# Two fp32r token parts in place of three bf16 ones for the experts' gather, a reordered router, and the late modulation's columns by 32-wide sums

## The chip, the cores and the metric

The kernel runs on one core of one Trainium2 chip. A core has the matrix engine TensorE (PE in the profile, with its weight loads as PEld), VectorE (DVE), ScalarE (ACT), GpSimd (POOL) and SyncE (SP), which issues almost all transfers. The metric is the time of one execution on the device in microseconds (us). It is compared as a median of runs.

## The reference

One block of a diffusion model over 256 latent tokens of width 1024, with 256 context tokens:

```python
m_lat = ada_mod(c, ada_w, ada_b)            # silu(c) @ w + b: six rows of 1024
h_lat = modulate(rms_norm(x, norm1_g), m_lat[0], m_lat[1])
y_lat = token_mixers(h_lat, h_ctx, ...)     # retention and latent attention, merged, @ w_out
x  = x + m_lat[2] * y_lat                   # gate 1
h2 = modulate(rms_norm(x, norm2_g), m_lat[3], m_lat[4])
x  = x + m_lat[5] * moe(h2, router_w, router_b, w_gu, b_gu, w_down, b_down)
return rms_norm(x, final_norm_g)

def moe(tok, ...):
    logits = tok @ router_w + router_b      # 32 experts
    top_val, top_idx = lax.top_k(logits, 4); gates = softmax(top_val)
    # each expert: gu = xb @ w_gu + b_gu; ((up + 1) * gate * sigmoid(1.702 * gate)) @ w_down + b_down
    # its tokens' outputs are weighted by the gates and added
```

All weights and activations are float32. Each of the 32 experts reads 12.6 MB of weights, some 403 MB in all.

## The kernel before, in words

**The order of work.** The kernel is one long list of `step`s, written out by hand, and the order in the list is the order on every engine. A step may name a weight tile. `run_steps` then loads that tile through SP, up to seven tiles (`WR`) ahead, into a ring of 512 KB tiles. Most products outside the experts are made of three fp32r products (fp32r is a 4-byte format of reduced precision, which the matrix engine takes directly). ACT and DVE split a weight tile into a high and a low fp32r part (`split`, lines 276 and 277, tile `ws`), two tiles ahead of its use. `mm3` (lines 285 to 287) multiplies high by high, high by low, low by high.

**The front (to about 545 us).** First comes the early modulation with the first projections, then four pairs of attention heads. In a pair, `scores` is followed by `attend_rows` (transposes of the probabilities on PE, split by ACT and DVE into `pth`/`ptl` and `kn`) and `attend` (their products with the values). The list goes on with the attention's branch product (`w_branch_mla`), four retention heads, their branch products, and `w_out`. In between lie 32 steps of `more_ada`. Each loads 512 KB of the late modulation's weights and adds them into the tile `ada` by one DVE instruction (line 340). `ada` then holds 128 partial rows that still have to be summed over the partitions.

**The late modulation (`gates`).** PE sums over the partitions by a product with ones. Two rows come out as copies on all partitions (lines 1190 and 1195: `gate1`, `gate2`). The shift and scale rows are wanted as columns, and 16 products of one column each make them (line 1201). `router_weights` folds them into the router's weights (line 1210).

**The router.** `residual(c)` makes half `c` of the new `x` on DVE. `x2_rows(c)` squares it (ACT), transposes it (PE) for the router's product (`router(c)`, line 1289), and starts the split of `x` into three bf16 parts (`split3`): ACT rounds and POOL subtracts, twice. `keep_warm` is idle work for PE. After that DVE alone works through a chain: the norm's inverse root (`rsqrt`), the logits `lgt`, the top four (`sel`, `eq`, the scan `cum`, `selb`), the tokens' positions `posm`, and a 0/1 matrix `oh` that says which token sits in which of an expert's 64 slots.

**The experts.** Weights come through a second ring of ten 2 MB tiles. Three open late in the retention (`open_ring`), one in `close_early`, five when the front's memory is given back, and the last when the pool `tmp` is. Per expert PE runs `gate_up` (line 1479, four tiles), `slot_rows` (line 1448), for every second expert `slot_scale` (line 1411), one `gather` (line 1426: `oh` times the three parts of `x`, for a later pair of experts), the transposes of the activation (line 145), `gu_bias` (line 1340), `down` (line 1510, two tiles), and `combine` (line 1459). The activation itself is a chain DVE, ACT, DVE (lines 1483 to 1487) between `gate_up` and those transposes.

Of the kernel before, what the change touches and what calls it, by code (L numbers as in the profile page):

```python
# [59 lines left out]
def hybrid_block(ctx: ExitStack, tc: tile.TileContext, A, out, dbg=None):  # L60
# [68 lines left out]
    identb = cst.tile([128, 128], BF, name="identb")  # L129
    nc.vector.tensor_scalar(identb, jp, 0.0, None, op0=OP.is_equal)  # L130
# [1024 lines left out]
    def open_late():  # L1155
# [13 lines left out]
        O["x3"] = late.tile([128, 2, D], BF, name="x3")  # L1169
# [11 lines left out]
    def open_out():  # L1181
        ret.close()
        dump("merged", M["acc"])
        O["tmp"] = enter(tmps, "tmp", side="right", reuse_waits="tile")

    def gates():
        mod2 = O["mod2"]
        for i in range(2):
            ps = pt_()
            nc.tensor.matmul(ps, one32[:, 0:1].to_broadcast([128, 128]), ada[:, 0, 512 * i:512 * i + 512],  # L1190
                             start=True, stop=True)
            nc.scalar.activation(O["gate1"][i], ps, AF.Copy)
        ps = pt_()
        for i in range(2):
            nc.tensor.matmul(ps[64 * i:64 * i + 64], one32[:, 0:1].to_broadcast([128, 64]),
                             ada[:, 1, 1024 + 512 * i:1536 + 512 * i], start=True, stop=True)
# [5 lines left out]
        nc.vector.scalar_tensor_tensor(mod2[:, 0], pc[:, 0], 1.0, g2c, op0=OP.add, op1=OP.mult)  # L1202
        nc.vector.tensor_copy(mod2[:, 1], pc[:, 1])
# [43 lines left out]
    def x2_rows(c):  # L1247
        x, tmp = O["x"], O["tmp"]
        cs = slice(512 * c, 512 * c + 512)
        if c == 0:  # L1250
            O["s2"] = O["late"].tile([128, 2, 2], F32, name="s2")
            x12 = accp.tile([128, 2, 2, D], BF, name="acc_m")
            O["xs"] = x12[:, 0], x12[:, 1], O["x3"]
# [4 lines left out]
        for t in range(2):  # L1258
# [3 lines left out]
            dst = tmp.tile([128, 4, 128], F32, name="x2T", bufs=2)  # L1262
            if c:
                nc.vector.tensor_copy(dst, ps)
            else:
                nc.scalar.activation(dst, ps, AF.Copy)
            O["x2T", c, t] = dst
        for t in range(2):
            O["split", c, t] = split3([p[:, t, cs] for p in O["xs"]], x[:, t, cs],
                                      tmp.tile([128, 512], F32, name="rest", bufs=2))  # L1270

    def split3(parts, src, rest):

        nc.scalar.activation(parts[0], src, AF.Copy)
        nc.gpsimd.tensor_tensor(rest, src, parts[0], op=OP.subtract)

        def more():
            nc.scalar.activation(parts[1], rest, AF.Copy)
            nc.gpsimd.tensor_tensor(parts[2], rest, parts[1], op=OP.subtract)
        return more  # L1280

    def split_more(c):
        for t in range(2):
            O["split", c, t]()

    def router(c):
        for t in range(2):
# [15 lines left out]
    step(lambda: router(0))  # L1303
    step(lambda: split_more(0))
# [6 lines left out]
    split_more(1)  # L1311
# [20 lines left out]
    r23 = late.tile([128, 3, 2], BF, name="r23")  # L1332
    split3([r23[:, i] for i in range(3)], r2, late.tile([128, 2], F32, name="r2r"))()
# [41 lines left out]
    keep_warm(CLK[7])  # L1375
    posm = late.tile([128, 2, E], F32, name="posm")
    nc.vector.scalar_tensor_tensor(posm, pp[:, 0:2], 1.0, selb, op0=OP.add, op1=OP.mult)
    nc.vector.tensor_scalar(posm, posm, -1.0, None, op0=OP.add)
    def oh_tile():
        return late.tile([128, 2, EG, CAP], BF, name="oh", bufs=2)  # L1380

    oh0 = oh_tile()
    one_hot(oh0, posm[:, :, 0:EG], EG)

# [20 lines left out]
    def slot_scale(oh, ne):  # L1405
# [3 lines left out]
        for t in range(2):  # L1409
            for i in range(3):  # L1410
                nc.tensor.matmul(ps[:, :w], r23[:, i, t:t + 1].to_broadcast([128, 128]),
                                 oh[:, t, :ne].rearrange("p e s -> p (e s)"), start=(t + i == 0), stop=(t + i == 3))
# [4 lines left out]
    def gather(oh, rb, xg, k4, ne):  # L1417
# [3 lines left out]
        for t in range(2):  # L1421
            rhs = oh[:, t, :ne].rearrange("p e s -> p (e s)")
            for p, part in enumerate(xs):
                for i in range(4):
                    k = 4 * k4 + i
                    nc.tensor.matmul(ps[:, i, :w], pairs(part[:, t], 4)[:, k // 2, k % 2], rhs, start=(t + p + i == 0), stop=(t + p == 3),  # L1426
                                     skip_group_check=True)
# [14 lines left out]
    def slot_rows(oh, i):  # L1442
# [3 lines left out]
        for t in range(2):  # L1446
            for h in range(2):
                nc.tensor.matmul(ps[64 * h:64 * h + 64, 128 * t:128 * t + 128], oh[:, t, i], identb,
# [265 lines left out]
```

## Time and profile before

| What | Value |
|---|---|
| median of 3 runs | 1489.52 us (1488.69 to 1493.41) |
| the profiled execution's own time | 1487.58 us |
| its span, first to last instruction | 1485.8 us |
| PE busy | 1388.0 us (93%) |
| DVE, ACT, POOL busy | 651.5, 344.4, 87.9 us |
| the chain that ended last | PE 51%, DMA 40%, DVE 6% of the span |
| traffic | 492.38 MB, mean 331 GB/s |
| mean granted clock of TensorE | 0.988 of full speed |

All times inside the kernel are counted from the span's start. The own time is 1.8 us longer than the span, which is what lies around it. The shares are means over two very different stages, the front and the experts, so each stage is read by itself. A matmul's busy time in the trace includes a modelled end, so the pace of a stream of matmuls is read from the distance between starts.

### The profile page before, as it was taken

The page shows a single profiled execution, that of the slowest core. Times are in us where ns is not written, and L with a number is a line of the kernel's source. Part 1 is how long each engine was busy: PE and PEld are TensorE (multiplying, and loading weights), DVE is VectorE, ACT ScalarE, POOL GpSimd, SP SyncE. Part 2 cuts the span into 40 slices and gives each one's busy share as a digit, 9 for nine tenths or more (in the row PEclk, how much of TensorE's full clock was granted, in tenths as well). Part 3 has the DMA queues.
Part 4 walks back from the last instruction along what each step waited for, and adds up shares of the span by engine and source line. Part 5 has one row for each costly group of instructions (what it writes and reads, how often), then busy time and mean ns, then how long its engine had stood idle before and what let it go on. Part 6 is the DMA issues. An engine that isn't in the chain of part 4 may idle for free.

```text
span 1485.8 us, 18943 instructions
## 1 busy us (share of the span) xinstructions
PE 1388.0 (93%) x7859; PEld 775.8 (52%) x7859; DVE 651.5 (44%) x1111; ACT 344.4 (23%) x604; POOL 87.9 (6%) x95
## 2 busy tenths in 40 slices
PE   8998999999999989999999999989899889989986
PEld 4677888888888874333333333333333333333323
DVE  4488876757676572323322323222322232223224
ACT  4364543534443331110100101100110011001001
POOL 2201050101101030000000000000000000000000
PEclk9999999999999899999999999999999999999998
DMA  8634473554548778999999999999999999999994
GB/s 286 204 108 141 142 265 101 164 177 130 176 161 322 266 286 337 427 426 427 428 425 428 427 426 427 427 428 426 427 428 426 428 427 427 427 428 427 427 422 172
DMA packets 75077, 492.38 MB, mean 331 GB/s; under 512 B 6579, under 2 KB 16892, under 8 KB 50152
## 3 DMA queue, kind: packets, MB, share of 16 engines
q1 hardware_dynamic: 74008, 489.22, 81.8%
q0 software_dynamic: 576, 1.23, 0.3%
q8 instruction: 63, 1.03, 0.3%
q10 hardware_dynamic: 400, 0.66, 0.1%
q14 instruction: 30, 0.25, 0.0%
HBM read 490.03 MB, written 1.05 MB: 331 GB/s over the span
## 4 chain that ended last, share of the span: by engine, by line
PE 51%; DMA 40%; DVE 6%; issue 1%; ACT 1%; POOL 0%; SPq 0%; DVEq 0%; ACTq 0%
DMA w<-in_exp_w_gu_dram 26%; DMA w<-in_exp_w_down_dram 13%; PE ps L1479 11%; PE ps L286 9%; PE ps L287 9%; PE ps L285 9%; PE ps L1510 5%; PE ps L145 2%; PE ps L1340 1%; PE ps L308 1%; PE ps L1459 1%; PE ps L457 1%; DVE up L1487 1%; DVE up L1485 1%; DVE ws L277 0%
## 5 line engine op out<-in xcount | busy, mean ns | idle before, releaser
L1479 PE MATMUL ps<-w,xg 128*64 128x512 f32 x2048 | 459.8, 596 | 36.2 <-DMA w<-in_exp_w_gu_dram 33.9
L1479 PEld LDWEIGHTS ps<-w,xg 128*64 128x64 f32 x2048 | 140.5, 137 | 333.8 <-issue 253.7
L1510 PE MATMUL ps<-w,ga 128*64 128x512 f32 x992 | 218.1, 592 | 0.0
L277 DVE TENSOR_TENSOR ws<-w,ws 128x1024 fp32r<-128x1024 f32 (+2 forms) x114 | 139.2, 1230 | 66.4 <-ACT ws L276 65.3
L1466 DVE SCALAR_TENSOR_TENSOR x<-ps,gate,x 128x512 f32<-128x512 f32 x124 | 84.5, 744 | 187.2 <-PE ps L1459 187.2
L1510 PEld LDWEIGHTS ps<-w,ga 128*64 128x64 f32 x992 | 71.2, 137 | 141.9 <-issue 141.9
L1519 DVE TENSOR_TENSOR ps<-ps,gate 128x512 f32<-128x512 f32 (+1 forms) x33 | 22.6, 683 | 270.1 <-PE ps L1510 261.2
L276 ACT ACTIVATE ws<-w 128x1024 fp32r<-128x1024 f32 (+2 forms) x114 | 116.9, 1028 | 101.0 <-PE ps L287 79.5
L1484 ACT ACTIVATE ps<-ga 128x512 f32<-128x512 f32 x32 | 19.3, 602 | 471.5 <-DVE ga L1483 471.5
L286 PE MATMUL ps<-ws,hh 128*128 128x512 f32 (+3 forms) x304 | 109.5, 360 | 3.5 <-DVE ws L277 3.5
L285 PE MATMUL ps<-ws,hh 128*128 128x512 f32 (+3 forms) x304 | 110.1, 362 | 2.4 <-DVE ptl L282 2.4
L287 PE MATMUL ps<-ws,hl 128*128 128x512 f32 (+3 forms) x304 | 109.1, 359 | 0.4 <-DVE hl L383 0.4
L1483 DVE TENSOR_SCALAR ga<-ps 128x512 f32<-128x512 f32 x32 | 22.1, 692 | 161.4 <-PE ps L1479 161.4
L281 ACT ACTIVATE up<-ps 128x512 fp32r<-128x512 f32 (+1 forms) x33 | 19.3, 584 | 260.2 <-DVE ps L1519 260.1
L286 PEld LDWEIGHTS ps<-ws,hh 128*128 128x128 f32 x304 | 57.3, 188 | 13.2 <-DVE ws L277 4.9
L1340 PE MATMUL ps<-bgu,ident 128*64 128x512 f32 x256 | 63.2, 615 | 0.0
L285 PEld LDWEIGHTS ps<-ws,hh 128*128 128x128 f32 x304 | 57.1, 188 | 11.4 <-DVE ptl L282 2.7
L287 PEld LDWEIGHTS ps<-ws,hl 128*128 128x128 f32 x304 | 57.1, 188 | 9.1 <-DVE hl L383 0.7
L145 PE MATMUL ps<-ident,up 128*128 128x128 f32 x128 | 24.1, 312 | 24.0 <-DVE up L1487 24.0
L340 DVE SCALAR_TENSOR_TENSOR ada<-w,sc,ada 128x1024 f32<-128x1024 f32 x32 | 40.6, 1278 | 0.0
L1426 PE MATMUL ps<-oh,acc_m 128*128 128x128 bf16 x512 | 40.6, 224 | 0.0
L285 PE MATMUL ps<-ath,hth 128*128 128x256 f32 x128 | 35.7, 279 | 1.2 <-ACT ath L281 1.2
(383 smaller groups left out, 1820.5 us busy)
## 6 DMA issues: line engine op xcount, KB each, us to landing
w<-in_exp_w_gu_dram SPq DMA_DIRECT2D x124, 2048.0 KB, 39.1
w<-in_exp_w_down_dram SPq DMA_DIRECT2D x62, 2048.0 KB, 39.1
w<-in_ada_w_dram SPq DMA_DIRECT2D x48, 512.0 KB, 4.5
w<-in_w_in_dram SPq DMA_DIRECT2D x48, 512.0 KB, 4.5
w<-in_w_in_dram SPq DMA_DIRECT2D x32, 256.0 KB, 4.3
w<-in_w_branch_ret_dram SPq DMA_DIRECT2D x16, 512.0 KB, 5.9
w<-in_exp_w_gu_dram SPq DMA_DIRECT2D x8, 1024.0 KB, 27.1
w<-in_w_branch_mla_dram SPq DMA_DIRECT2D x8, 512.0 KB, 5.2
```

The lines of the kernel that those rows point to most:

```text
L145: nc.tensor.transpose(dst, src, ident[:n, :n])
L276: nc.scalar.activation(hi[:, :n], src, AF.Copy)
L277: nc.vector.tensor_tensor(lo[:, :n], src, hi[:, :n].bitcast(F32), op=OP.subtract)
L285: nc.tensor.matmul(ps, a[0], b[0], start=start, stop=False, skip_group_check=True)
L286: nc.tensor.matmul(ps, a[0], b[1], start=False, stop=False, skip_group_check=True)
L287: nc.tensor.matmul(ps, a[1], b[0], start=False, stop=stop, skip_group_check=True)
L340: nc.vector.scalar_tensor_tensor(a, w, sc[:, k:k + 1], a, op0=OP.mult, op1=OP.add)
L1340: nc.tensor.matmul(ps[64 * h:64 * h + 64], pick_row(c // 512).to_broadcast([128, CAP]), bgu, start=True, stop=False, skip_group_check=True)
L1426: nc.tensor.matmul(ps[:, i, :w], pairs(part[:, t], 4)[:, k // 2, k % 2], rhs, start=(t + p + i == 0), stop=(t + p == 3), skip_group_check= ...
L1466: nc.vector.scalar_tensor_tensor(a, pss[h], g[:, t:t + 1], a, op0=OP.mult, op1=OP.add)
L1479: nc.tensor.matmul(ps[64 * h:64 * h + 64], xg[k // 4][:, k % 4, sl], w[:, c:c + 512], start=False, stop=(k == KD - 1), skip_group_check=True)
L1510: nc.tensor.matmul(py[64 * h:64 * h + 64], hT[f], w[:, 1024 * r + 512 * h:1024 * r + 512 * h + 512], start=(f == 0), stop=(f == KD - 1))
```

## The change

**Gather.** `x` is kept as two fp32r parts, `acc_m` (high, in place of two bf16 parts) and a new tile `xlo` (low, 8 KB per partition in place of 4 KB for `x3`). The subtraction is a DVE instruction; POOL no longer takes part. `oh` and the inverse norm's parts `r2s` are fp32r too. A `gather` has 16 products in place of 24, a `slot_scale` 4 in place of 6. `slot_rows` multiplies by the float32 identity.

**Router.** The squares, the transposes and the router's products of half 0 are interleaved with the transposes of half 1; ACT makes all four copies `x2T`, and the low parts of half 1 are made later, among the position work. The product of the bias rows with `gate2` goes from POOL to DVE.

**Late modulation.** Four sums of 32 equal rows each (one product per 512 columns) are stacked in one tile, copied by ACT and transposed four times; a column of the result is picked out. The `more_ada` steps stand at other places: per attention pair 1 in place of 3, per branch step of the attention 1 in place of 1 in two, per retention head 5 in place of 4.

```diff
@@ attention pairs @@
         fill(FILL[2 * pair])
-        more_ada(2)
         step(attend_rows)
...
         fill(FILL[2 * pair + 1])
+        more_ada(1)
         step(lambda pair=pair: attend(pair))
-        more_ada(1)
@@ branch product of the attention @@
             matmul2(("bm0", "bm1"), "w_branch_mla", 256 * k2, 512 * c, lambda: M["mT"], 2 * k2, k2 == 0, k2 == 3)
-            if k2 % 2:
-                more_ada(1)
+            more_ada(1)
@@ retention heads, ahead of the query and key projection @@
+        more_ada(1)
         if h == 0:
@@ gates @@
+        rows = pt_()
+        for g, part in enumerate((ada[:, 1, 0:512], ada[:, 1, 512:1024], ada[:, 0, 1024:1536], ada[:, 0, 1536:2048])):
+            nc.tensor.matmul(rows[32 * g:32 * g + 32], one32, part, start=True, stop=True)
+        row = O["late"].tile([128, 512], F32, name="xg", bufs=3)
+        nc.scalar.activation(row, rows, AF.Copy)
...
-        pc = pt_((128, 2, KD))
-        for i, part in enumerate((ada[:, 1, 0:1024], ada[:, 0, 1024:2048])):
-            for k in range(KD):
-                nc.tensor.matmul(pc[:, i, k:k + 1], pairs(part, 4)[:, k // 2, k % 2], one32[:, 0:1], start=True, stop=True)
...
+        pc = pt_((128, 4, 4, 32))
+        for c in range(4):
+            transpose(pc[:, c].rearrange("p a b -> p (a b)"), pairs(row, 2)[:, c // 2, c % 2])
@@ x2_rows @@
+        def high(t):
+            nc.scalar.activation(hi[:, t, cs], x[:, t, cs], AF.Copy)
+
+        def low(t):
+            nc.vector.tensor_tensor(lo[:, t, cs], x[:, t, cs], hi[:, t, cs].bitcast(F32), op=OP.subtract)
+
+        if c == 0:
+            for f in (high, low, turned, square):
+                for t in range(2):
+                    f(t)
+        else:
+            for t in range(2):
+                square(t)
+                turned(t)
+                router(0, (t,))
+            for t in range(2):
+                high(t)
+            O["rest"] = [lambda t=t: low(t) for t in range(2)]
...
-    step(lambda: router(0))
-    step(lambda: split_more(0))
     step(lambda: residual(1))
...
-    split_more(1)
@@ after the top four @@
     keep_warm(CLK[7])
+    O["rest"][0]()
...
     one_hot(oh0, posm[:, :, 0:EG], EG)
+    O["rest"][1]()
@@ gather @@
-        for t in range(2):
-            rhs = oh[:, t, :ne].rearrange("p e s -> p (e s)")
-            for p, part in enumerate(xs):
+        for p, part in enumerate(xs):
+            for t in range(2):
+                rhs = oh[:, t, :ne].rearrange("p e s -> p (e s)")
                 for i in range(4):
...
-        nc.gpsimd.tensor_tensor(bdn[r], bdn[r], gate2[r], op=OP.mult)
+        nc.vector.tensor_tensor(bdn[r], bdn[r], gate2[r], op=OP.mult)
```

**What stands where on the engines.** First DVE's queue at the first attention pair, from the split of the next weight tiles to that of the attention's output (`w<-ps`); `ada` is a step of the late modulation, `ptl` and `kn` are the low parts of the probabilities. Before:

```order
L277 TENSOR_TENSOR ws<-w_1114,ws 128x1024
L340 SCALAR_TENSOR_TENSOR ada<-w_960,sc,ada 128x1024
L340 SCALAR_TENSOR_TENSOR ada<-w_988,sc,ada 128x1024
L282 TENSOR_TENSOR ptl<-ps,pth 128x4x128 x2
L282 TENSOR_TENSOR kn<-ps,kn 128x4x128 x2
L680 TENSOR_TENSOR qr<-ps,qr 64x512
L277 TENSOR_TENSOR ws<-w_1208,ws 128x768
L282 TENSOR_TENSOR w<-ps,w 128x256 x2
L340 SCALAR_TENSOR_TENSOR ada<-w_1057,sc,ada 128x1024
```

And with the change:

```order
L275 TENSOR_TENSOR ws<-w_1016,ws 128x1024
L280 TENSOR_TENSOR ptl<-ps,pth 128x4x128 x2
L280 TENSOR_TENSOR kn<-ps,kn 128x4x128 x2
L678 TENSOR_TENSOR qr<-ps,qr 64x512
L275 TENSOR_TENSOR ws<-w_1055,ws 128x768
L338 SCALAR_TENSOR_TENSOR ada<-w_986,sc,ada 128x1024
L280 TENSOR_TENSOR w<-ps,w 128x256 x2
```

Two `ada` steps ahead of `ptl` are gone, and the third stands ahead of the output's split. The other pairs read alike.

Second PE's queue in `gates` and after it, up to the last retention branch (`ath`); `r` are the retention's rows, `ct` the router's weights. Before:

```order
L1190 MATMUL ps<-ada,one_148 128x512 x2
L1195 MATMUL ps<-ada,one_148 64x512 x2
L1201 MATMUL ps<-one_148,ada 128x1 x16
L145 MATMUL ps<-ident,r 128x128 x8
L1210 MATMUL ps<-ct,mod_4741 128x32 x8
L285 MATMUL ps<-ws,ath 128x512
```

And with the change:

```order
L1187 MATMUL ps<-ada,one_146 32x512 x4
L1192 MATMUL ps<-ada,one_146 128x512 x2
L1197 MATMUL ps<-ada,one_146 64x512 x2
L143 MATMUL ps<-ident,xg 128x128 x4
L143 MATMUL ps<-ident,r 128x128 x8
L1213 MATMUL ps<-ct,mod_4739 128x32 x8
```

The 16 products of one column have become 4 sums ahead of the rest and 4 transposes at their place.

Third the router, from the last transfer that POOL issues there (`rbias`) to the copies of the gates (`ga`). POOL before:

```order
L1165 DMA rbias<-in_router_b_dram 128x32
L1275 TENSOR_TENSOR rest<-x,acc_m 128x512 x2
L1279 TENSOR_TENSOR x_4744<-rest,acc_m 128x512 x2
L1275 TENSOR_TENSOR rest<-x,acc_m 128x512 x2
L1279 TENSOR_TENSOR x_4744<-rest,acc_m 128x512 x2
L1275 TENSOR_TENSOR r2r<-r_5255,r_5277 128x2
L1279 TENSOR_TENSOR r_5277<-r2r,r_5277 128x2
L1544 TENSOR_TENSOR xg<-xg,gate_4740 32x512 x2
L1551 COPY ga<-gate 128x2x32 x4
```

With the change POOL has one small instruction between those two, and DVE has the low parts: here DVE's queue from the scan `cum` to the first two `oh`.

```order
L1365 SCALAR_TENSOR_TENSOR cum<-one_146,above,eq 128x32 x2
L1366 SCALAR_TENSOR_TENSOR eq<-cum,eq 128x64
L1367 TENSOR_TENSOR selb<-sel,eq 128x64
L1274 TENSOR_TENSOR xlo<-x,acc_m 128x512
L1379 SCALAR_TENSOR_TENSOR posm<-ps,selb 128x64
L1380 TENSOR_SCALAR posm<-posm 128x64
L1320 TENSOR_TENSOR oh<-posm,slot 128x256
L1274 TENSOR_TENSOR xlo<-x,acc_m 128x512
L1392 TENSOR_SCALAR negm<-m_5286 128x2
L1320 TENSOR_TENSOR oh<-posm,slot 128x256
```

Eight 128x512 subtractions have left POOL's queue at the router, and two 128x512 subtractions now stand among DVE's position work; two more stand earlier, ahead of `residual(1)`.

## Rows read from the trace of the kernel before

**Rows 1.** Windows: length, busy PE, PEld, DVE, ACT, POOL; clock, DMA share, GB/s.

```profile
555.50:565.00 9.50, 9.50 (x72) 5.89 (x71) 3.24 (x10) 1.82 (x5) 0.76 (x4) 0.83 0.21 61
700.00:800.00 100.00, 96.85 (x554) 38.36 (x552) 31.42 (x52) 11.18 (x25) 0.00 (x0) 1.00 1.01 426
```

**Rows 2.** Waits of PE, whole span: us in total, times, longest.

```profile
PE ps L1479 <- DMA w<-in_exp_w_gu_dram: 33.9, 33, 1.3
...
PE ps L286 <- DVE ptl L282: 3.7, 2, 2.9
...
PE ps L285 <- DVE ptl L282: 2.4, 1, 2.4
```

**Rows 3.** Timeline of SP at the experts' begin: start, us, what.

```profile
563.27 3.76 SPq L1112 DMA_DIRECT2D w<-in_exp_w_down_dram  x2
```

**Rows 4.** Chain that ended last, at the experts: start, us, what.

```profile
586.31 1.45 PE ps L1426 x24
...
614.93 6.87 PE ps L1479 x32
...
641.74 6.87 PE ps L1479 x32
```

**Rows 5.** Timeline of PE, behind one expert's last gate_up and at the last expert.

```profile
737.43 0.28 PE L1448 MATMUL ps<-identb,oh 128*64 128x128 bf16 x4
...
739.92 0.75 PE L145 MATMUL ps<-ident,up 128*128 128x128 f32 x4 [0.43 <-DVE up L1487]
...
1443.38 7.03 PE L1479 MATMUL ps<-w,xg 128*64 128x512 f32 x32
```

**Rows 6.** Timeline of DVE, second attention pair: two late-modulation steps.

```profile
139.20 2.47 DVE L340 SCALAR_TENSOR_TENSOR ada<-w,sc,ada 128x1024 f32<-128x1024 f32 x2
```

**Rows 7.** Windows: part of the attention's branch product.

```profile
200.00:210.00 10.00, 10.00 (x44) 8.08 (x43) 8.35 (x8) 3.88 (x4) 8.89 (x15) 1.00 0.92 309
```

**Rows 8.** Timeline of PE in `gates` and behind it.

```profile
487.98 1.88 PE L1190 MATMUL ps<-ada,one 128*128 128x512 f32 x4
490.79 4.47 PE L1201 MATMUL ps<-one,ada 128*128 128x1 f32 x32
...
496.86 3.46 PE L1210 MATMUL ps<-ct,mod 128*128 128x32 f32 x16
```

**Rows 9.** Windows: two stretches behind `gates`.

```profile
494.00:504.00 10.00, 10.00 (x40) 9.23 (x40) 3.28 (x7) 2.14 (x3) 0.00 (x0) 0.50 0.59 231
505.00:513.00 8.00, 8.00 (x37) 6.56 (x36) 6.17 (x7) 3.18 (x3) 0.00 (x0) 1.00 0.27 90
```

**Rows 10.** Timeline of DVE, then of POOL, at the router.

```profile
545.77 2.20 DVE L166 SCALAR_TENSOR_TENSOR rs_t<-r,rs_w 128x1 f32<-128x1 f32 x2
...
548.08 0.34 DVE L166 SCALAR_TENSOR_TENSOR rs_t<-r,rs_w 128x1 f32<-128x1 f32 x2
...
549.06 0.41 DVE L1329 SCALAR_TENSOR_TENSOR lgt<-ps,r,rbias 128x32 f32<-128x32 f32 x2
...
551.65 1.14 DVE L1365 SCALAR_TENSOR_TENSOR eq<-cum,eq 128x64 f32<-128x64 f32 x1
...
545.68 2.27 POOL L1279 TENSOR_TENSOR x<-rest,acc_m 128x512 bf16<-128x512 f32 x2
...
550.11 2.60 POOL L1544 TENSOR_TENSOR xg<-xg,gate 32x512 f32<-32x512 f32 x2
```

**Rows 11.** Timeline of PE from the router's second half to the first expert.

```profile
543.07 1.92 PE L1289 MATMUL ps<-ct,x2T 128*128 128x32 f32 x16
...
553.10 0.19 PE L1370 MATMUL ps<-selb,upper 128*128 128x32 bf16 x1 [5.24 <-DVE selb L1366]
...
559.58 4.51 PE L1479 MATMUL ps<-w,xg 128*64 128x512 f32 x20
```

**Rows 12.** Timeline of PE in the retention: two neighbouring fp32r products.

```profile
480.10 0.28 PE L285 MATMUL ps<-ath,hth 128*128 128x256 f32 x1
480.21 0.28 PE L286 MATMUL ps<-atl,hth 128*128 128x256 f32 x1
```

More of the change, by code (lines that the diff above doesn't have):

```diff
@@ L1168, in open_late @@
         O["gate1"] = [late.tile([128, 512], F32, name="xg", bufs=3) for _ in range(2)]
-        O["x3"] = late.tile([128, 2, D], BF, name="x3")
     def close_early():
@@ L1183, in open_out @@
         dump("merged", M["acc"])
+        O["xlo"] = enter(ctx, "xl", side="right", reuse_waits="tile").tile([128, 2, D], F32R, name="xlo")
         O["tmp"] = enter(tmps, "tmp", side="right", reuse_waits="tile")
@@ L1197, in gates @@
         nc.scalar.activation(O["gate2"], ps, AF.Copy)
-        pc = pt_((128, 2, KD))
-        for i, part in enumerate((ada[:, 1, 0:1024], ada[:, 0, 1024:2048])):
-            for k in range(KD):
-                nc.tensor.matmul(pc[:, i, k:k + 1], pairs(part, 4)[:, k // 2, k % 2], one32[:, 0:1], start=True, stop=True)
-        nc.vector.scalar_tensor_tensor(mod2[:, 0], pc[:, 0], 1.0, g2c, op0=OP.add, op1=OP.mult)
-        nc.vector.tensor_copy(mod2[:, 1], pc[:, 1])
+        pc = pt_((128, 4, 4, 32))
+        for c in range(4):
+            transpose(pc[:, c].rearrange("p a b -> p (a b)"), pairs(row, 2)[:, c // 2, c % 2])
+        for g in range(2):
+            nc.vector.scalar_tensor_tensor(mod2[:, 0, 4 * g:4 * g + 4], pc[:, :, g, 0], 1.0, g2c[:, 4 * g:4 * g + 4],
+                                           op0=OP.add, op1=OP.mult)
+            nc.vector.tensor_copy(mod2[:, 1, 4 * g:4 * g + 4], pc[:, :, 2 + g, 0])
     def router_weights():
@@ L1251, in x2_rows, with square, turned @@
             O["s2"] = O["late"].tile([128, 2, 2], F32, name="s2")
-            x12 = accp.tile([128, 2, 2, D], BF, name="acc_m")
-            O["xs"] = x12[:, 0], x12[:, 1], O["x3"]
+            O["xs"] = accp.tile([128, 2, D], F32R, name="acc_m"), O["xlo"]
             bank("lg", shape=(128, 2, E))
-        for t in range(2):
+        hi, lo = O["xs"]
+        def square(t):
             junk = tmp.tile([128, 512], F32, name="jk")
             nc.scalar.activation(junk, x[:, t, cs], AF.Square, accum_out=O["s2"][:, t, c:c + 1])
-        for t in range(2):
+        def turned(t):
             ps = pt_((128, 4, 128))
@@ L1261, in x2_rows, with router @@
                 transpose(ps[:, j], pairs(x[:, t, cs], 2)[:, j // 2, j % 2])
[L1262 to L1287, printed above, removed]
+            dst = O["x2T", c, t] = tmp.tile([128, 4, 128], F32, name="x2T", bufs=4)
+            nc.scalar.activation(dst, ps, AF.Copy)
+        def high(t):
[14 more added lines that the diff above has]
+            O["rest"] = [lambda t=t: low(t) for t in range(2)]
+    def router(c, ts=range(2)):
+        for t in ts:
             for j in range(4):
@@ L1331, in hybrid_block @@
     xs = O["xs"]
-    r23 = late.tile([128, 3, 2], BF, name="r23")
-    split3([r23[:, i] for i in range(3)], r2, late.tile([128, 2], F32, name="r2r"))()
+    r2s = late.tile([128, 2, 2], F32R, name="r2s")
+    nc.scalar.activation(r2s[:, 0], r2, AF.Copy)
+    nc.gpsimd.tensor_tensor(r2s[:, 1], r2, r2s[:, 0].bitcast(F32), op=OP.subtract)
     def gu_bias(pick_row):
@@ L1379, in oh_tile @@
     def oh_tile():
-        return late.tile([128, 2, EG, CAP], BF, name="oh", bufs=2)
+        return late.tile([128, 2, EG, CAP], F32R, name="oh", bufs=2)
     oh0 = oh_tile()
     one_hot(oh0, posm[:, :, 0:EG], EG)
+    O["rest"][1]()
     gt1 = late.tile([128, 2, E], F32, name="gate")
@@ L1409, in slot_scale @@
         for t in range(2):
-            for i in range(3):
-                nc.tensor.matmul(ps[:, :w], r23[:, i, t:t + 1].to_broadcast([128, 128]),
-                                 oh[:, t, :ne].rearrange("p e s -> p (e s)"), start=(t + i == 0), stop=(t + i == 3))
+            for i in range(2):
+                nc.tensor.matmul(ps[:, :w], r2s[:, i, t:t + 1].to_broadcast([128, 128]),
+                                 oh[:, t, :ne].rearrange("p e s -> p (e s)"), start=(t + i == 0), stop=(t + i == 2))
         rb = xp.tile([128, EG * CAP], F32, name="rb")
@@ L1420, in gather @@
         ps = pt_((128, 4, EG * CAP))
-        for t in range(2):
-            rhs = oh[:, t, :ne].rearrange("p e s -> p (e s)")
-            for p, part in enumerate(xs):
+        for p, part in enumerate(xs):
+            for t in range(2):
+                rhs = oh[:, t, :ne].rearrange("p e s -> p (e s)")
                 for i in range(4):
                     k = 4 * k4 + i
-                    nc.tensor.matmul(ps[:, i, :w], pairs(part[:, t], 4)[:, k // 2, k % 2], rhs, start=(t + p + i == 0), stop=(t + p == 3),
-                                     skip_group_check=True)
+                    nc.tensor.matmul(ps[:, i, :w], pairs(part[:, t], 4)[:, k // 2, k % 2], rhs,
+                                     start=(t + p + i == 0), stop=(t + p == 2), skip_group_check=True)
         n = xg[:, :, :w]
@@ L1447, in slot_rows @@
             for h in range(2):
-                nc.tensor.matmul(ps[64 * h:64 * h + 64, 128 * t:128 * t + 128], oh[:, t, i], identb,
+                nc.tensor.matmul(ps[64 * h:64 * h + 64, 128 * t:128 * t + 128], oh[:, t, i].bitcast(F32), ident,
                                  start=True, stop=True)
```

2 lines of the change are left out of this document (removed).

## Prediction

> **What bounds the kernel now.** I read the views in this order: the windows, the waits of PE, the chain that ended last, then the timelines at the places that the change touches.
>
> The experts' stage is bound by transfers. DMA is busy all the time there at 426 GB/s [rows 1], and PE waits 33 times for gate and up weights [rows 2]. One expert is 12.58 MB, so it takes 12.58 MB / 426 GB/s = 29.5 us. PE alone needs 641.74 - 614.93 = 26.8 us [rows 4]. PE's work in this stage is free up to 2.7 us per expert. What counts is when the stream of transfers gets going for good.
>
> That moment is set by PE. In the 9.5 us from 555.5 the DMA share is only 0.21 [rows 1]: all ten weight tiles are loaded, none is used up yet. The first expert begins at 559.58 [rows 11], its first tile is free one quarter of `gate_up` later, and SP issues the next transfer at 563.27 [rows 3]. The hole is (1 - 0.21) x 9.5 = 7.5 us. An earlier first expert ends it earlier, and so everything behind it.
>
> In the front PE is busy nearly all the time. Its few waits are for DVE [rows 2, 11]. Time that PE saves there moves the weight tiles' release and the first expert alike.
>
> **Part 1: late-modulation steps leave the attention pairs.** Two of them cost DVE 2.47 us ahead of `ptl` in every pair [rows 6]. PE waits for `ptl` three times, 2.4 + 3.7 = 6.1 us, the longest 2.9 [rows 2]. Without the two steps `ptl` comes up to 2.47 us earlier, so the gain is at most 2.4 + 2.47 + (3.7 - 2.9) = 5.7 us. The third step still stands in the pair, behind `ptl`, where the output's split is not urgent. I take 5.5 us; the bounds are 0 (another wait takes their place) and 5.7.
>
> The steps go to two places. In the attention's branch product each of eight steps gets a 512 KB load and 1.24 us of DVE work (half of 2.47). Before, the eight steps hold four. DVE is busy 8.35 of 10 us there, DMA 0.92 at 309 GB/s [rows 7], and a step takes about 2.8 us of PE (12 products of 512 columns at 0.23 us, twice the distance in [rows 12]). Four more DVE instructions are 5.0 us in 22 us, of which 22 x 0.165 = 3.6 us are idle; four more loads are 2.1 MB or 6.8 us at 309 GB/s, of which 1.8 us are idle. The cover is the lead: weights are split two tiles ahead (5.6 us of PE), loads run seven tiles ahead, and the pairs before it have fewer loads now. If the cover held nothing the stage would lose 5 us. I take 0.5 us. In the retention heads one more step each is 1.24 us of DVE in some 65 us; PE is full there and DVE is not, so it costs nothing.
>
> **Part 2: `gates`.** The 16 one-column products go: 4.47 us [rows 8]. Four sums, 32 columns wide each, come. Two full-width ones take 1.88 us [rows 8], so 0.94 each. Products on part of the array run side by side: `gate_up` has 16 of half width and 512 columns in 6.87 us [rows 4], 0.43 each. The four therefore cost between 0.94 (all side by side) and 3.76 us (none); I take 1.0. Four transposes come, and four fp32r-sized loads of 128 columns bound them by 4 x 0.11 = 0.44 us [rows 12]. ACT's copy lies behind `gate1` and `gate2` on PE. Net: 4.47 - 1.0 - 0.5 = 3.0 us.
>
> More lies in the clock. From 494 to 504 it is at half (0.50, the 1.2 GHz level, 40 matmul records in 10 us), and from 505 at full (1.00, 37 records of full-size products in 8 us) [rows 9]. It fell about 3 us after the one-column products began. At half clock stand eight transposes, the router's weight product (3.46 us, where 16 such records take 1.92 us at full clock [rows 8, 11]), and ten branch products. The branch products take 0.43 in place of 0.23, the transposes twice their time. That is 1.5 + 2.0 + 0.9 = 4.4 us. With the one-column products gone, what the engine did before the fall is gone; between the full-size sums and the branch products stand twelve transposes and the weight product alone. I expect the clock to stay. Gain 3.0 + 4.4 = 7.4, less about 0.9 because the retention's rows and then the columns come from DVE a little late: 6.5 us. Bounds: 0.2 us (sums one after another, clock falls anyway) and 7.4.
>
> **Part 3: the router chain.** PE waits 5.24 us for `selb` until 553.10 [rows 11]. That is the most this wait can give, since PE's own work ahead of it is the same: eight transposes, 16 router products, bias rows and idle products. The logits were made at 549.06 [rows 10] though the router's second half was through at 543.07 + 1.92 = 545.0 [rows 11]. They waited for the inverse root, and that for POOL: a DVE instruction on 128x1 took 2.20 us for two while POOL subtracted for 2.27, and 0.34 us right after [rows 10]. Likewise 1.14 us for `eq` beside POOL's bias product of 2.60. With POOL's work gone and ACT making the copies `x2T`, the root is ready before 545.0, so the logits gain 4.0 us. `selb` came 553.10 - 549.06 = 4.0 us behind them, of which the two scans and `eq` are stretched; I take 2.3 us, so 547.3, before PE's queue is there (553.10 - 5.24 = 547.9). The wait goes entirely, 5.2 us; if the chain kept its 4.0 us, it would give 4.1. The low part of half 1 adds a 128x512 DVE instruction (about 0.7 us; 1.24 is the price of twice that) between `selb` and `posm`; it lies beside PE's count products, and the second stands behind `oh`.
>
> From 553.10 to the first expert pass 6.48 us [rows 11], of which 54 bf16 products (six and 48) fill about 5.2. The change has four and 32 fp32r ones. No row shows an fp32r product with 128 columns. With 256 columns the distance is 0.11 us [rows 12]; a narrower one cannot need more if it passes the array once, and PE no longer goes idle before them, which leaves the clock up. 36 x 0.115 = 4.1, gain 1.1. If 128 columns pass four times, each is a quarter of a full-width float32 sum of 0.94, so 0.235, and 36 x 0.235 = 8.5 us lose 3.3. I take the first, since every fp32r stream here runs once through. The first expert gains 5.2 + 1.1 = 6.3 us, within the hole of 7.5.
>
> **Part 4: the experts' PE work.** `gather` had 24 products in 1.45 us [rows 4]; 16 at 0.115 are 1.8. They and `slot_rows` stand between `gate_up` and the transposes, where PE has 739.92 - 737.43 = 2.49 us, 0.43 of them idle, because the activation's chain is not ready sooner [rows 5]. So they cost nothing or a few tenths, against 2.7 us that are free per expert.
>
> Here the Trainium skill speaks against the change: "TensorE: Matmul & The Clock Gate", section "Weight-path perf modes — Fast Weight Load (FWL) and DoubleRow", says that weights are loaded fast when there are 128 of them and their type is not FP32, and its section on LDWEIGHTS gives columns / 1.2 ns, an estimate of 107 ns, for the plain load. By that the gather of 16 would take 1.7 us in place of 1.45: a third fewer products, and no gain on PE. The rows above give 1.8.
>
> **The sum.** The profiled execution's own time is 1487.58 us, and 5.5 - 0.5 + 6.5 + 6.3 = 17.8 us come off: 1469.8. The median of the runs stands 1.9 above that execution and the lowest 1.1; I add 1.5 and predict 1471 us.
>
> **The rivals.** *Four passes (chance 0.32).* An fp32r product of 128 columns costs 0.235 us. The first expert gains 1.9 (5.2 - 3.3) only. A gather is 3.8 us in place of 1.45, `slot_rows` and every other `slot_scale` add 0.4, and of these 2.7 us the idle 0.43 (second experts) to about twice that (the others, which have no `slot_scale`) are free: a PE round grows by 2.0 to 28.8 us. The last expert then begins 31 x 28.8 = 893 us behind the first, at 559.6 - 13.4 + 893 = 1439, against 1443.4 now [rows 5]: 4 us faster, 1485 us, and 3 us per 0.1 us of a round to either side. For it speaks that no stream here is that narrow; against it, that nothing but float32 is slow here. The Trainium skill's page "FP8 and Floating Point Precision" (TensorE Precision Notes) names four passes for true FP32 alone; no run here shows it for fp32r.
>
> *The front gains little (0.09).* The stalls of parts 1 and 2 come back as waits for weights, or the clock falls anyway: only part 3 and 2 us are left, 8.3 in all, 1481 us.
>
> *PE becomes the bound (0.07), the other side.* Each narrow product costs as much as a one-column float32 one, 4.47 / 16 = 0.28 us [rows 8]. A round becomes 26.8 + 16 x 0.28 + 1.1 - 1.45 - 0.4 = 30.5 us. Above 29.5 it decides. The last expert begins 946 us after the first, at about 1494 against 1443: 1540 us.
>
> *Nothing moves (0.07).* DMA ends the kernel and the hole is filled by another wait, the last ring tile's or SP's: 1489 us, within 0.3%.
>
> **Chances and range.** 0.45 for the forecast, whose own range is 1466 to 1477. From 1466 (all bounds at their best) to 1488 lie the forecast, the small gain and most of the four passes; what is left out is PE as the bound, most of the case that nothing moves, and the four passes with a round near 29 us. Under 0.3% (4.5 us) no change can be told. Faster: 0.45 + 0.09 + 0.20 of the four passes = 0.74. The same: 0.08 of the four passes and 0.06, 0.14. Slower: 0.12.
>
> **What would show it.** Right: no `ptl` waits; clock 1.00 throughout from 488 to 513 in its new place; no PE wait for `selb`; tiny DVE instructions at 0.2 to 0.4 us; the low DMA share before the first expert down to 1 to 2 us; fp32r gather starts 0.11 us apart. Wrong: starts 0.23 apart, new waits of PE for `ws` in the branch product, a clock of 0.50 behind `gates`, or PE waiting for DMA no longer in the experts.

## The result and the profile after

| What | Before | With the change |
|---|---|---|
| median | 1490.93 us (15 runs, 1488.28 to 1496.73) | 1480.38 us (15 runs, 1475.58 to 1487.67) |
| ratio | | 0.9935, 95% interval 0.9920 to 0.9949 |
| profiled execution, own time and span | 1487.58, 1485.8 us | 1479.33, 1477.5 us |

The kernel became faster, by 0.65% where 1.2% were forecast. In the profiled executions 8.25 us came off in place of 17.8. Where they came off is read from the starts of the same PE instructions in the two timelines:

| PE instruction | Before | After | Difference | Since the row above |
|---|---|---|---|---|
| first product with `ptl`, last attention pair | 189.47 | 183.20 | -6.27 | pairs: -6.3 |
| third product of head 0's first tile, behind the branch product | 215.17 | 214.02 | -1.15 | branch product: +5.1 |
| first product with `ath` in head 0 | 243.61 | 245.00 | +1.39 | head 0: +2.5 |
| third product behind `r_rows` in head 1 | 277.20 | 281.37 | +4.17 | half clock: +2.8 |
| last product ahead of `gates` | 487.74 | 492.09 | +4.35 | heads 1 to 3: +0.2 |
| a product of the last retention branch, at full clock in both | 505.30 | 502.77 | -2.53 | `gates`: -6.9 |
| router's second half | 543.07 | 540.71 | -2.36 | `w_out`: +0.2 |
| first product with `selb` | 553.10 | 545.34 | -7.76 | router chain: -5.4 |
| first expert's `gate_up` | 559.58 | 551.07 | -8.51 | first gather: -0.8 |

Behind that the experts run as before, with DMA at 427 GB/s throughout: in both traces the rounds from the second to about the fifteenth go at PE's own pace (26.8 to 27.2 us each, while the tiles loaded ahead are used up), and the later ones at that of the transfers (mostly 29 to 30 us). The end lies 8.3 us earlier. The waits of PE over the whole span (us in total, times, longest; line numbers are 2 or 3 off against those of before) show the same in short. First some lines of the kernel before, then those with the change:

```profile
PE ps L145 <- DVE up L1487: 24.0, 31, 2.3
...
PE ps L286 <- DVE ws L277: 3.5, 4, 1.5
...
PE ps L285 <- ACT ath L281: 1.2, 2, 0.8
PE ps L286 <- DVE atl L282: 0.7, 2, 0.4
```

```profile
PE ps L1482 <- DMA w<-in_exp_w_gu_dram: 30.5, 34, 1.7
PE ps L284 <- DVE ws L275: 6.6, 8, 1.5
...
PE ps L143 <- DVE up L1490: 2.0, 1, 2.0
PE ps L283 <- ACT ath L279: 1.3, 1, 1.3
...
PE ps L1414 <- DVE oh L1320: 0.6, 1, 0.6
...
PE ps L284 <- DVE ptl L280: 0.5, 1, 0.5
```

Of the waits for `ptl` [rows 2] 0.5 us is left, and the wait for `selb` [rows 11] is gone. The waits for `ws` have grown from 3.5 to 6.6 us. The experts' waits for `up` fell from 24.0 to 2.0 us, as the longer gather and `slot_rows` now fill that gap. The windows that answer to [rows 1, 7, 9], columns as there:

```profile
205.00:215.00 10.00, 7.39 (x30) 5.11 (x29) 6.00 (x6) 3.18 (x3) 3.14 (x2) 1.00 0.82 266
246.00:252.00 6.00, 5.85 (x26) 5.27 (x26) 2.17 (x3) 0.86 (x2) 0.46 (x1) 0.50 0.46 142
496.00:504.00 8.00, 8.00 (x50) 6.91 (x49) 4.71 (x12) 3.72 (x6) 0.00 (x0) 1.00 0.99 390
554.00:564.00 10.00, 10.00 (x48) 3.28 (x46) 0.09 (x1) 0.38 (x1) 0.00 (x0) 1.00 0.85 326
700.00:800.00 100.00, 99.90 (x528) 41.84 (x526) 30.47 (x50) 12.33 (x26) 0.00 (x0) 1.00 1.01 427
```

PE is idle for 2.6 of 10 us in the branch product, and a stretch at half clock stands where head 0 begins. Behind `gates` the clock is 1.00. The hole in the transfers ahead of the first expert is down to (1 - 0.85) x 10 = 1.5 us. PE's timeline in `gates` and behind it, which answers to [rows 8]:

```profile
492.42 1.06 PE L1187 MATMUL ps<-ada,one 128*32 128x512 f32 x8
493.42 1.98 PE L1192 MATMUL ps<-ada,one 128*128 128x512 f32 x4
...
496.34 0.75 PE L143 MATMUL ps<-ident,xg 128*128 128x128 f32 x4
496.92 1.04 PE L143 MATMUL ps<-ident,r 128*128 128x128 f32 x8
497.79 1.87 PE L1213 MATMUL ps<-ct,mod 128*128 128x32 f32 x16
```

The four 32-wide sums take 1.0 us together, so they ran side by side. The router's weights take 1.87 us in place of 3.46.

### The profile page after: what moved, and what is told of

The parts are those of the page before. It is cut to its first block, busy times and chain, and to the rows that moved or that the text cites. A ratio compares the mean times of both kernels' runs of the same rounds, so it can differ in the third digit from the quotient of the medians.

```text
span 1477.5 us, 18567 instructions
## 1 busy us (share of the span) xinstructions
PE 1409.6 (95%) x7679; PEld 798.1 (54%) x7679; DVE 650.9 (44%) x1116; ACT 347.4 (24%) x602; POOL 71.5 (5%) x84
## 4 chain that ended last, share of the span: by engine, by line
PE 53%; DMA 39%; DVE 5%; ACT 1%; issue 1%; POOL 0%; SPq 0%; ACTq 0%; DVEq 0%
DMA w<-in_exp_w_gu_dram 25%; DMA w<-in_exp_w_down_dram 13%; PE ps L1482 11%; PE ps L284 8%; PE ps L285 8%; PE ps L283 8%; PE ps L1513 6%; PE ps L143 2%; PE ps L1341 2%; PE ps L306 1%; PE ps L1429 1%; PE ps L1462 1%; PE ps L455 1%; DVE ws L275 1%; DMA w<-in_w_branch_mla_dram 1%
## 5 line engine op out<-in xcount | busy, mean ns | idle before, releaser
L1482 PE MATMUL ps<-w,xg 128*64 128x512 f32 x2048 | 459.6, 595 | 32.3 <-DMA w<-in_exp_w_gu_dram 30.5
L284 PE MATMUL ps<-atl,hth 128*128 128x256 f32 x128 | 37.1, 290 | 0.5 <-DVE atl L280 0.4
L285 PE MATMUL ps<-ath,htl 128*128 128x256 f32 x128 | 36.9, 288 | 0.0
```

Source lines behind the costliest of these rows:

```text
L284: nc.tensor.matmul(ps, a[0], b[1], start=False, stop=False, skip_group_check=True)
L285: nc.tensor.matmul(ps, a[1], b[0], start=False, stop=stop, skip_group_check=True)
L1482: nc.tensor.matmul(ps[64 * h:64 * h + 64], xg[k // 4][:, k % 4, sl], w[:, c:c + 512], start=False, stop=(k == KD - 1), skip_group_check=True)
```

## The experiments

All ratios are to the kernel before, run on the same chip. The change itself has 0.9935.

**1. Part 1 alone, and all but part 1.** Only the places of `more_ada` differ, as in the diff ahead: first the old kernel with the new places, then the new kernel with the old ones.

> The kernel before, with the late-modulation steps alone moved to their new places; nothing else of the change. Theory A (the lost time sits in part 1): the attention pairs gain about 6 us, the attention's branch product gives 5.0 back because a weight tile, its split and the release of a late-modulation tile form a loop that is longer than PE's step, head 0 gives 2.7 more (one more late-modulation instruction ahead of the split of `ath`), and a stretch of half clock behind these waits costs 2.8. Sum: +4.2 us on 1490.9, about 1495, a ratio of 1.003. Theory B (the forecast's part 1, and the loss sits elsewhere): -5.0, about 1486, 0.9966. Theory C (the half-clock stretch is an accident of one execution): +1.4, 1492, 1.001.

> The changed kernel with the late-modulation steps put back to their old places; parts 2 to 4 stay. Theory A: 4.2 us faster than the changed kernel, 1480.4 - 4.2 = 1476, a ratio to the kernel before of 0.990; waits for `ptl` return (6.1 us) and waits for `ws` in the branch product vanish, clock 1.00 from 244 to 252 us. Theory B: about 5 us slower than the changed kernel, 1485, 0.9965. Theory C: 1479, 0.992.

Measured: alone 1488.20 us, 0.9981 (0.9969 to 0.9993); undone 1482.81, 0.9951 (0.9927 to 0.9974). So the moved steps alone gain 2.7 us by the medians, half of what I forecast. The undone kernel is 2.4 us slower than the change by the medians, but its interval overlaps the change's (0.9920 to 0.9949), so it shows neither a gain nor a loss. Neither run shows the loss that theory A read out of one pair of traces. The trace of the first has A's picture all the same (of what the pairs gave 1.5 us are left behind the branch product, and the clock is at half from 245 to 252 us), but its execution took 1491.2, 3 us above the median of its 12. Single executions differ by several us, and A had taken the half clock that one of them showed for a constant.

The price of the new places is steady, though. From the first `ptl` product of the last pair to the third product behind the branch product it is 25.7 us in both traces with the old places and 30.8 to 31.3 in the five with the change's (the change, `part1_alone`, and experiments 4, 5 and 6). From there to head 0's first product with `ath` it is 28.4 us in both, and 30.1 to 31.7 in the five. The trace of the undone kernel shows the old waits back:

```profile
PE ps L284 <- DVE ptl L280: 3.7, 2, 2.9
PE ps L283 <- DVE ptl L280: 2.4, 1, 2.4
PE ps L284 <- DVE ws L275: 2.1, 2, 1.5
```

**2. Where the branch product loses.** VectorE is busy for only 6 of 10 us there (above), and DMA moves 266 GB/s at a share of 0.82, so neither is full. The timelines of SP, ACT and DVE in the changed kernel show a loop. The last line is SP's wait for the late-modulation instructions from 180 to 225 us:

```profile
201.93 0.37 SPq L265 DMA_DIRECT2D w<-in_w_branch_mla_dram  x1
202.39 3.75 SPq L265 DMA_DIRECT2D w<-in_ada_w_dram  x2
```

```profile
206.13 1.06 ACT L274 ACTIVATE ws<-w 128x1024 fp32r<-128x1024 f32 x1 [2.81 <-DMA w<-in_w_branch_mla_dram]
```

```profile
199.48 1.23 DVE L275 TENSOR_TENSOR ws<-w,ws 128x1024 fp32r<-128x1024 f32 x1 [1.57 <-ACT ws L274]
200.62 1.28 DVE L338 SCALAR_TENSOR_TENSOR ada<-w,sc,ada 128x1024 f32<-128x1024 f32 x1
...
203.35 1.22 DVE L275 TENSOR_TENSOR ws<-w,ws 128x1024 fp32r<-128x1024 f32 x1 [0.25 <-ACT ws L274]
204.49 1.28 DVE L338 SCALAR_TENSOR_TENSOR ada<-w,sc,ada 128x1024 f32<-128x1024 f32 x1
207.22 1.23 DVE L275 TENSOR_TENSOR ws<-w,ws 128x1024 fp32r<-128x1024 f32 x1 [1.46 <-ACT ws L274]
```

```profile
SPq L265 <- DVE ada L338: 23.2, 9, 3.2
```

The late-modulation instruction ends at 200.62 + 1.28 = 201.90, its tile of the ring is free, and SP issues the next weight tile at 201.93. ACT waits for that tile until 206.13 and splits it, DVE follows at 207.22, and only behind that stands the next but one late-modulation instruction. Two branch steps thus take 7.8 us, 3.9 each, where PE needs 2.8. In this experiment three of the four added steps load elsewhere, into attention tiles that are no longer used:

```diff
+    side = [lambda n=n: M["mp"].tile([128, 4, 256], F32, name=n).rearrange("p a b -> p (a b)") for n in ("pth", "ptl", "mvh")]
...
-            more_ada(1)
+            more_ada(1, side.pop(0) if k2 % 2 == 0 and (c, k2) != (0, 0) else wtile4)
```

> The changed kernel; of the eight late-modulation steps in the attention's branch product three of the four added ones load into dead attention tiles (`pth`, `ptl`, `mvh`) and no longer take a tile of the ring. VectorE's work, the bytes and the order of instructions stay the same. Theory A1 (the loop release of the late-modulation tile - transfer - split - next late-modulation instruction): the period of 3.9 us per branch step falls to PE's 2.8, the waits of PE for `ws` there go nearly to nothing, 4 to 5 us gained at the branch product; if the clock stays up behind it, up to 7.5 in all: 1473 to 1476, a ratio of 0.988 to 0.990. Theory A2 (VectorE's load of 1.24 us per added step is the limit, or the bandwidth of the transfers): period still 3.9, no gain, 0.9935.

Measured: 1475.85 us, 0.9904 (0.9885 to 0.9924), at the far end of A1's range. VectorE's rows, and a window:

```profile
194.71 1.23 DVE L275 TENSOR_TENSOR ws<-w,ws 128x1024 fp32r<-128x1024 f32 x1 [1.88 <-ACT ws L274]
...
201.31 1.22 DVE L275 TENSOR_TENSOR ws<-w,ws 128x1024 fp32r<-128x1024 f32 x1
...
209.31 1.22 DVE L275 TENSOR_TENSOR ws<-w,ws 128x1024 fp32r<-128x1024 f32 x1
```

```profile
195.00:205.00 10.00, 9.75 (x42) 7.56 (x41) 9.37 (x10) 3.18 (x3) 5.67 (x8) 1.00 0.98 354
```

The period is now (209.31 - 194.71) / 5 = 2.9 us. VectorE is fuller than before, 9.37 of 10 us, and PE hardly waits. The stretch from the last pair to behind the branch product, 30.8 us in the change, takes 26.2. That is 4.6 us less, as much as the two ratios differ by (0.9904 and 0.9935; their intervals just touch). So the loop through the ring was the limit, not VectorE's load, and A2 falls.

**3. Other places for the steps.** First four in the branch product, three in head 0 and seven in each later head; then the ring left as in the change, with two of head 0's five steps moved to heads 1 and 2; then this together with the side tiles. The diff is the second one's. `head0_only` was run last of all, and "the last kernel" in what was expected of it is `side_and_head0`.

```diff
-        more_ada(1)
+        if h:
+            more_ada(1)
         if h == 0:
             qk(range(0, 2))
...
             branch(h - 1, 0, add_branch(h - 1))
+            if h < RH - 1:
+                more_ada(1)
...
-        more_ada(1)
+        if h:
+            more_ada(1)
         step(ret_scores)
```

> The changed kernel with the late-modulation steps placed otherwise: attention pairs 1 each as in the change, branch product 4 as before, retention head 0 has 3 (none ahead of the split of `ath`), heads 1 to 3 have 7 each. Theory A: all of the loss of part 1 goes and about 1 us of the old waits for `ath` in head 0 too; the attention pairs keep their 6.3: 5.0 + 2.7 + 2.8 + 1 = 11 us faster than the changed kernel if heads 1 to 3 hide 7 steps each (2 or 3 more of 1.24 us on VectorE in 65 us), 1469 to 1471, a ratio of 0.986. Theory B (loss elsewhere): no more than 0.5 us faster than the changed kernel, 0.993. If the heads do not hide them: new waits of PE for `ws` there, about 1.2 us for each step that is not hidden.

> The changed kernel with only the second of the two edits of the last kernel: two of head 0's five late-modulation steps moved to heads 1 and 2, the branch product as in the change (all tiles from the ring). Theory A (two separate losses, the ring's loop in the branch product and the two instructions ahead of `ath` in head 0): the waits for `ws` in the branch product stay at 3 to 4 us, 2 to 2.5 us come back in head 0, and up to 2.8 more if the clock no longer falls there: 1475.5 to 1478, a ratio of 0.9905 to 0.992. Theory B (one loss: what head 0 loses is the branch product's lateness carried on): no gain, 1480.4, 0.9935.

> The kernel with three late-modulation tiles beside the ring, and besides this two of head 0's five steps, those that stand ahead of the split of `ath`, moved to heads 1 and 2, each behind the first half of the branch product. Theory A (each of the two delays `ath` in head 0 by 1.2 us while PE waits for it; heads 1 and 2 hide one step more): 2 us faster than with the tiles beside the ring alone, 1473 to 1474, a ratio of 0.989; up to 1.7 more if the half-clock stretch at 240 us goes. Theory B (the waits move on to the next split): 1475.9, 0.9904. If heads 1 and 2 do not hide the sixth step: up to 1.2 us slower for each.

| Kernel | Median | Ratio |
|---|---|---|
| `heads_later` | 1477.63 us | 0.9898 (0.9877 to 0.9919) |
| `head0_only` | 1475.20 us | 0.9898 (0.9877 to 0.9919) |
| `side_and_head0` | 1471.63 us | 0.9877 (0.9862 to 0.9893) |

Against the change's 0.9935 the tiles beside the ring give 0.0031, head 0 gives 0.0037 (a little more than expected), both 0.0058. So theory B, no gain, falls for `head0_only`. That the two losses are separate is shown only in part. Between `side_and_head0` and either of the other two the intervals overlap. From the last pair's first `ptl` product to head 0's first `ath` the change takes 61.8 us, the side tiles alone 55.9, `head0_only` 56.9, both 54.4, and the kernel before 54.1: 5 to 6 us each, 7.4 together. The best kernel, `side_and_head0`, beats the change by about 8.6 us by the ratios and stands where I had forecast the change, but with one step fewer in head 0 than even the kernel before. Waits of PE in `head0_only` from 195 to 256 us, where the change has 3.8 us for the two parts of `ws`, 0.4 for `atl`, 1.3 for `ath` and 1.3 more in head 0 (`w`, `gth`, `htl`):

```profile
PE ps L284 <- DVE ws L275: 2.3, 4, 0.8
PE ps L284 <- DVE atl L280: 0.7, 2, 0.4
PE ps L283 <- ACT ath L279: 0.4, 1, 0.4
```

Head 0 is freed though the branch product still stalls (by less than the 3 to 4 us expected), and this execution shows no half clock in the front. In `heads_later` theory A's gain in head 0 came, but seven steps per later head are too many, and 1469 to 1471 us were missed: its trace is 8.5 us ahead of the change's at the rows of head 1 and only 3.2 at the router's weights, with these waits of PE from 230 to 495 us:

```profile
PE ps L284 <- DVE ws L275: 2.3, 2, 1.2
PE ps L1218 <- DMA ct<-in_router_w_dram: 1.9, 1, 1.9
```

**4. `gates` as before.** The 16 one-column products are back, the rest of the change stays.

> The changed kernel with the late modulation's columns made as before (16 products of one column, no 32-wide sums, no transposes); all else of the change stays. Theory A (part 2 is worth what the trace shows, 3.0 us of work and 3 to 4 us of half clock): PE reaches the router's chain 6 us later, about 1486, a ratio of 0.997; the granted clock falls to 0.50 behind the one-column products. Theory B (the clock falls somewhere in this stretch in many executions anyway): 3 us slower than the changed kernel, 1483, 0.9955. Theory C (nothing there is on the path): 1480.4, 0.9935.

Measured: 1486.45 us, 0.9978 (0.9969 to 0.9987), as theory A has it. PE's timeline and a window:

```profile
496.37 3.99 PE L1198 MATMUL ps<-one,ada 128*128 128x1 f32 x32
500.23 1.95 PE L143 MATMUL ps<-ident,r 128*128 128x128 f32 x8
501.97 3.46 PE L1207 MATMUL ps<-ct,mod 128*128 128x32 f32 x16
```

```profile
500.00:510.00 10.00, 10.00 (x38) 9.02 (x38) 3.28 (x7) 2.14 (x3) 0.00 (x0) 0.50 0.62 232
```

**5. GpSimd's work at the router.** Five subtractions that nothing reads:

```diff
+            pz = tmp.tile([128, 512], F32, name="pz")
+            for t in (0, 1, 0, 1, 0):
+                nc.gpsimd.tensor_tensor(pz, x[:, t, cs], x[:, t, 0:512], op=OP.subtract)
```

> The changed kernel with five more subtractions of 128x512 on GpSimd into a tile that nothing reads, beginning when the second half of the new x is there; nothing waits for them but the closing of their pool. Theory A (GpSimd's elementwise work stretches VectorE's small instructions): those of the inverse root take 0.8 to 1.1 us each in place of 0.17, the logits come 2 to 3 us later and PE waits 1.5 to 3 us for `selb` again; about 2 us slower than the changed kernel, 1482.5, 0.995. Theory B (before the change the chain was late because something waited for GpSimd's results): rows of the root as in the changed kernel, no wait for `selb`, 1480.4, 0.9935.

Measured: 1485.66 us, 0.9970 (0.9955 to 0.9984). The timelines of POOL and DVE:

```profile
542.28 5.34 POOL L1289 TENSOR_TENSOR pz<-x 128x512 f32<-128x512 f32 x4 [0.70 <-DVE x L1243]
```

```profile
543.69 1.25 DVE L154 TENSOR_SCALAR rs_w<-rs_v 128x2 f32<-128x2 f32 x1
...
545.04 1.37 DVE L164 SCALAR_TENSOR_TENSOR rs_t<-r,rs_w 128x1 f32<-128x1 f32 x2
546.33 1.30 DVE L167 SCALAR_TENSOR_TENSOR r<-rs_t,r 128x1 f32<-128x1 f32 x2
547.55 0.34 DVE L164 SCALAR_TENSOR_TENSOR rs_t<-r,rs_w 128x1 f32<-128x1 f32 x2
```

Until POOL ends at 547.62, two one-element instructions take 1.3 us together; right behind, 0.34. PE waits for `selb` again:

```profile
PE ps L1374 <- DVE selb L1370: 1.3, 1, 1.3
```

Theory A holds, though the run cost more than it said: 5 us, not 2. In its trace the chain from the router's second half to `selb` takes 6.1 us in place of 4.6, so POOL's work costs 1.4 there. The first gather then runs at half clock (553 to 563 us), which costs 2.8 more up to the first expert, and 4.0 us had been lost ahead of the chain, all of it behind `gates`. How the median's 5 us divide is not shown. The Trainium skill, "SBUF — State Buffer", section "SBUF: two separate sides", says that a GpSimd instruction and a VectorE instruction in a two-port mode, or with two SBUF inputs while the GpSimd one reads SBUF, share a pair of ports as an exclusive lock, and that whichever starts first holds it for its whole instruction. These rows agree: POOL's four instructions of 1.34 us, taken as equally long, end at 543.6, 545.0, 546.3 and 547.6, and the slow VectorE rows end at 544.9, 546.4 and 547.6.

**6. What is free in the experts.** The gather is issued twice over, so the tokens' rows come out doubled.

```diff
-        for p, part in enumerate(xs):
+        for n in range(4):
+            p, part = n % 2, xs[n % 2]
```

> The changed kernel with every `gather` issued twice over (32 products in place of 16; the tokens' rows come out doubled), 1.9 us more PE work per expert. Theory A (what is free per expert is the difference between the mean distance of the experts, (1443.38 - 559.58) / 31 = 28.5 us before the change, and PE's round of 27.2): the round becomes 29.1, the last expert begins 31 x 29.1 = 903 us behind the first, at 1454 against 1435, so about 17 us slower than the changed kernel, 1497, 1.004, and PE hardly waits for DMA any more. Theory B (as the forecast's part 4 put it, 2.5 us between gate_up and the transposes and 29.5 us of transfers per expert are cover enough): no more than 1 us slower, 1481.5, 0.994.

Measured: 1496.73 us, 1.0047 (1.0034 to 1.0060): theory A. PE's timeline of one round, without its middle:

```profile
712.48 7.09 PE L1483 MATMUL ps<-w,xg 128*64 128x512 f32 x32
...
719.93 1.16 PE L1430 MATMUL ps<-oh,acc_m 128*128 128x128 f32 x8
720.93 1.10 PE L1430 MATMUL ps<-oh,xlo 128*128 128x128 f32 x8
721.87 1.11 PE L1430 MATMUL ps<-oh,acc_m 128*128 128x128 f32 x8
722.82 1.11 PE L1430 MATMUL ps<-oh,xlo 128*128 128x128 f32 x8
...
741.15 7.09 PE L1483 MATMUL ps<-w,xg 128*64 128x512 f32 x32
```

The round is 28.7 us, and 29.1 with a `slot_scale`, just above the mean distance of 28.5. PE no longer waits for expert weights at all.

## Why the prediction was wrong

**The failed step is the cost of where part 1's steps went.** I wrote that the branch product's cover is its lead, seven tiles of loads and two of splits, and took 0.5 us; the pair of traces shows 5.1, and the others with these places 5.1 to 5.6, just above the 5 us of my own upper bound. One of the signs that I had named for being wrong, new waits of PE for `ws` there, is in the trace. I had counted VectorE's load and the bandwidth, and experiment 2 shows that neither decides. The lead is counted in ring tiles. With a late-modulation tile behind every weight tile, seven tiles are three and a half steps, and of these the split takes two. A weight tile comes free at its split, but a late-modulation tile only when its instruction has run, and SP's queue waits for it with the next weight tile behind it.

**"In the retention heads it costs nothing"** failed in head 0: the trace loses 2.5 us there (1.6 to 3.2 in the five traces), and experiment 3 gets 0.0037 (some 5 us) back with two steps moved, where the change had added one. I looked at the heads as a whole ("PE is full there and DVE is not"), where head 0 begins with waits for `ath` and `atl` already in the kernel before (1.2 and 0.7 us, above). The 2.8 us of half clock behind were in no term. These three make 10 us, the miss in the traces (17.8 against 8.25) with the smaller terms below. Only the first two are shown to come from the places of the steps.

**Right, with their sizes** (forecast, then the traces): the waits for `ptl` 5.5, 6.3; `gates` 6.5, 6.9, and 6 by experiment 4; the router chain 5.2, 5.4, and its mechanism by experiment 5; the first gather 1.1, 0.8, of which a new wait of 0.64 us for `oh` takes a part. Sixteen fp32r products of 128 columns start within 1.94 us (719.93 to 721.87 in experiment 6), 0.12 apart, so the rival of four passes falls, as do a PE that becomes the bound and a change that moves nothing. The Trainium skill, "TensorE: Matmul & The Clock Gate", section "LDWEIGHTS (loading the stationary operand)", gives columns / 1.2 ns for a weight load, by which the prediction estimated 1.7 us for these 16. My rows gave 1.8; the trace is a little above both.

**The rival that came closest** is the one that the front gains little, 1481 us, to which I gave 0.09: part 1's gain came back as waits for weights, as it says. Its other half, a loss in `gates`, did not come in this trace.

**Part 4** was right that the gather is hidden, but "2.7 us that are free per expert" was too much. By experiment 6, 1.9 us more already cost 17; what is free ends at the mean distance of the experts, 28.5 - 27.2 = 1.3 us. The 2.7 held only for the later experts: in about the first fifteen rounds PE sets the pace itself, and of its 30.5 us of waits for gate and up weights 30.3 come behind 970 us.

**Open** is what the half clock has to do with the places of the steps. Eight of the eleven traces have such a stretch in the front, between 113 and 254 us, and those of both kernels with the old places are among them (142 to 146 us in the kernel before). Three have none: `head0_only`, `side_and_head0` and the trace of experiment 5. Part 1's gain of 2.7 us by the medians is not in the traces, where the new places cost 7.2 to 8.3 us behind the pairs and the pairs give 5.6 to 6.8. The granted clocks on record bear on this: the executions of `part1_alone` had a mean of 0.989 and those of the kernel before on the same chip 0.986. At 0.988 alone they took 1487.9 (4 executions) and 1488.7 us (6) on average. So most of that gain goes with the clock, and no run shows whether the new places keep it up.

## What to carry to other kernels

- Where one queue issues loads into a ring in order, follow one tile round: its release, the issue, the landing, the split, and the instruction behind which the next release stands. If that loop, divided by the steps that it spans, is longer than a step, no engine and no bandwidth need be full for the stage to stall.
- A mean over a stage ("PE is full there and DVE is not") hides its first microseconds. Look at the place where an instruction is inserted, and at who waits behind it in the same queue.
- What is free beside a transfer-bound loop is the mean distance of its rounds less the round of the engine, not the gap that one sees inside a round.

## What the runs showed of the hardware

TensorE's clock falls to half (1.2 GHz) at other places in other executions of like code. Behind the old `gates` it fell in all three traces that have them. Behind the new `gates` it stayed up in six traces, the changed kernel's among them, and fell in two: that of experiment 5 (498.6 to 505.5 us) and that of `heads_later` (496.6 to 500.0). In these two alone PE had waited some 2 us for the router's weights just before; the line is from experiment 5, that of `heads_later` stands above:

```profile
PE ps L1213 <- DMA ct<-in_router_w_dram: 2.0, 1, 2.0
```

In the first gather it stayed up in the changed kernel and fell in the traces of four experiments (`part1_undone`, `heads_later`, and experiments 5 and 6). Ahead of it PE waits 0.6 us for `oh` in the changed kernel and in three of these four alike, so no row tells why.

The 15 executions of the changed kernel took 1475.6 to 1487.7 us, a spread as large as what the change gained. It goes in part with the clock: the three at a mean granted clock of 0.995 took 1475.6 to 1479.0 us, the two at 0.991 1483.5 and 1484.5.
